# Cross attention of a decoder layer: memory's parts beside w_out, key pair 0 ahead of the queries, w_co's first unit by heads, X2's squares in wide operations after w_co

## The chip, the cores and the metric

The kernel runs on one core of a Trainium2 chip. The metric is device time in microseconds (us) for one execution of the whole program, lower is better. Each of the core's engines runs its own queue of instructions in order: PE (matrix multiplies into banks of PSUM), DVE (vector operations), ACT (activation functions, casts), POOL (general vector operations, and a DMA queue of its own), and SP, which here only issues DMA transfers. An engine waits where an operand isn't ready or a buffer isn't free.

## The reference

One inference step of one decoder layer, for 256 prompt rows and 8 sample rows (one new row each) that share all weights, in fp32:

```python
# 1. mixer: sliding-window attention and an SSD (Mamba-2) group, then one output projection
x = x + concatenate([attn, ssd], -1) @ w_out               # 3072 -> 2048
# 2. cross attention, 4 heads of 128, into 256 memory tokens
h = rms_norm(mem, g_mem)                                   # 256 x 2048 (prompt only)
k = rms_norm((h @ w_ck).reshape(b, m, 4, 128), ck_norm_g)
v = (h @ w_cv).reshape(b, m, 4, 128)
q = rms_norm((rms_norm(x, g_cross) @ w_cq).reshape(b, t, 4, 128), cq_norm_g)
p = softmax(einsum('bqhd,bshd->bhqs', q, k) * 128 ** -0.5)
x = x + einsum('bhqs,bshd->bqhd', p, v).reshape(b, t, 512) @ w_co
# 3. ConvFFN
u = causal_dwconv(rms_norm(x, g_ffn) @ w_up, ...)          # 2048 -> 2 x 5632, width 3
x = x + (silu(gate) * val) @ w_down
```

The sample rows attend to cached memory keys and values of their own (`cache_mem_k`, `cache_mem_v`). Memory's keys and values, the SSD states and other caches are outputs too.

## The kernel before

**Tiling.** Activations lie transposed: 128 features on the partitions, 264 columns (256 prompt rows, then 8 sample rows), 16 such blocks for the 2048 features. Every fp32 product is three matmuls (`mm3`, lines 100 to 103): of the weights' high part with the activations' high part (L101) and low part (L102), and of the weights' low part with the activations' high part (L103). The high part is a rounded cast, the low part what it leaves. `split` (L91 to L98) makes both for activations: the high part on ACT, the low part on DVE.

**Weights.** `weights` (L69) loads 1 MB from HBM into one of two `wraw` slots over SP's queue; of each half, ACT casts `whi` (L86) and DVE subtracts `wlo` (L87), into four slots each, so the engines can be two units ahead of PE. `proj` (L105) runs some units of weights into `nb` PSUM banks and then hands each bank to an evaluation, which frees it. Of the banks, three are `mm`, two `t`, and `s`, `x` and `y` have one each.

**Order.** The program is written in one sequence; a scheduler decides at build time in which order each engine's queue gets its instructions, and `high_priority` marks weights and evaluations. After that the order is fixed.

**The stretch of the change**, in the order of the program (L736 to L979):
- `w_out` in two halves: eight units against `AT` (attention), then eight projections of two units against `Y` (the SSD group). Each evaluation of the second half adds to the residual `res`, splits the sum into `X1` (16 blocks, `x1h` and `x1l`) and adds its square to `accx` (`sumsq`, L173: ACT squares, POOL adds).
- `memory_norm` (L738): loads the memory into four `mraw` tiles of 128x1024, squares and adds its 16 blocks one by one (`accm`, by `sumsq`), and takes the inverse root mean squares `rmc` (`col_rms`, L188, whose small matmuls are at L192).
- After `w_out`: the 16 blocks of the memory are split into `M` (`mh`, `ml`).
- `q_pair(0)`, `q_pair(1)`: the queries of two heads each, with their per-head norms (`head_rms`, L798, small matmuls at L804), and the sample rows' queries sent to HBM (`dram_q`). `k_pair(0)` and `k_pair(1)`: memory's keys (`kx`).
- `sample_logits(i)`: the sample rows of head pair i. Cached keys `kt` are multiplied by the queries, which come back from HBM on all partitions (`qb`); the exponentials `es` go to HBM (`dram_p`).
- `probs(h)`: softmax of head h for the prompt rows (`e`, divided by `den` on POOL, transposed into `pts`).
- `v_pair(i)`: memory's values (`vx`). `sample_out(i)`: the exponentials come back on all partitions (`pb`), cached values `vt` (three slots) are multiplied by them; the result goes into the sample columns of `OH` and `OL`. `out_head(h)`: probabilities times values, into head h's prompt columns of `OH` and `OL`.
- `w_co`: four units of 1 MB, each with four output blocks (`nb=4`, all in `mm` banks) over the four heads. The evaluation adds to `res`, splits into `X2` (`x2h`, `x2l`) and adds the square to `accx2`.
- `r2`, from `accx2` (`total`, L181), which the evaluations of `w_up` need: each multiplies its bank by `r2` into `u` (L1033).
- Beside `w_up`, the SSD states of the sample rows are updated (`new_state`): 16 tiles `hn` of eight 128x128 updates, each in three slots: loaded over SP's queue, scaled on ACT (L1005), updated on DVE (L1006), and stored by POOL's queue. `w_up` and `w_dn` fill the time from 671 us to the end.

Of the kernel before, what the change touches and what calls it, by code (L numbers as in the profile page):

```python
# [14 lines left out]
D = 2048  # L15
# [32 lines left out]
def hybrid_decoder_step_kernel(ctx: ExitStack, tc: tile.TileContext, I, O):  # L48
# [56 lines left out]
    def proj(units, acts, evac, n=T, nb=2, tag="mm"):  # L105

        outs = [psum(tag) for _ in range(nb)]
        for ui, (src, (ah, al)) in enumerate(zip(units, acts)):
            parts = src if isinstance(src, list) else weights(src)
            for pi, (wh, wl) in enumerate(parts):  # L110
                wh = wh.rearrange("p (k c) -> p k c", c=128 * nb)
                wl = wl.rearrange("p (k c) -> p k c", c=128 * nb)
                nk = wh.shape[1]
                for m in range(nb):
                    for k in range(nk):
                        kk = pi * nk + k
                        mm3(outs[m][:, :n], wh[:, k, m * 128:(m + 1) * 128], wl[:, k, m * 128:(m + 1) * 128],
                            ah[:, kk, :n], al[:, kk, :n],
                            ui == 0 and kk == 0, ui == len(units) - 1 and kk == nk * len(parts) - 1)
        for m in range(nb):  # L120
            with tc.high_priority():
                evac(m, outs[m][:, :n])
# [615 lines left out]
    def memory_norm():  # L738
        cr = ExitStack()
        xp = cr.enter_context(tc.tile_pool(name="xp", bufs=1))  # L740
        accm = small.tile([128, T], F32, tag="acc", bufs=1, name="accm")[:, :TP]
        mraw = []
        for h in range(4):
            mr = xp.tile([128, 4, TP], F32, tag="mr", name="mraw", bufs=4)
            nc.sync.dma_start(out=mr, in_=I["memT"][:, 4 * h:4 * h + 4, :])
            for k in range(4):
                sumsq(accm, mr[:, k, :], h + k == 0, TP)
            mraw.append(mr)
        rmc = col_rms(accm, "rmc")
        return cr, xp, mraw, rmc  # L750

# [10 lines left out]
    cr, xp, mraw, rmc = memory_norm()  # L762
# [12 lines left out]
    r1c = col_rms(accx, "r1c")  # L775

    ax2 = cpool.tile([128, 8, 2], F32, name="ax2")
    V.tensor_copy(out=ax2, in_=accx[:, TP:T].unsqueeze(2).broadcast_to([128, 8, 2]))
    p = psum("y")
    PE.matmul(p[0:16, 0:1], ax2.rearrange("p b m -> p (b m)"), ones[:, 0:1], start=True, stop=True)  # L780
    r1s = cpool.tile([16, 2], F32, name="r1s")
    rms(r1s[:, 0:1], p[0:16, 0:1], D)
    V.tensor_tensor(out=r1s[:, 1:2], in0=r1s[:, 0:1], in1=r1s[:, 0:1], op=ALU.mult)


    M = [(T3(apool, 8, F32R, "B", f"mh{h}", 4), T3(apool, 8, F32R, "B", f"ml{h}", 4)) for h in range(2)]
    for k in range(KB):
        split(M[k // 8][0][:, k % 8, :TP], M[k // 8][1][:, k % 8, :TP], mraw[k // 4][:, k % 4, :], pc("g_mem", k))

    qx = xp.tile([128, 4, TP], F32, tag="mr", name="qx", bufs=4)  # L790
    kx = xp.tile([128, 4, TP], F32, tag="mr", name="kx", bufs=4)
    vx = xp.tile([128, 2, 512], F32, tag="mr", name="vx", bufs=4)
    pts = [xp.tile([128, 2, 2, 256], F32, tag="mr", name="pt0", bufs=4), xp.tile([128, 2, 2, 256], F32, name="pt1")]
    OH = xp.tile([128, 4, T], F32R, name="oh")
    OL = xp.tile([128, 4, T], F32R, name="ol")
# [14 lines left out]
    def q_pair(i):  # L810
# [18 lines left out]
        for m in range(2):  # L829
            P.tensor_copy(out=qq[:, :, m], in_=sqs[m][:, TP:T])  # L830
# [10 lines left out]
    def k_pair(i):  # L841
# [10 lines left out]
        proj([I["w_ck"][2 * i], I["w_ck"][2 * i + 1]], M, ev, n=TP)  # L852
# [36 lines left out]
    def sample_out(i):  # L889
        pbs = []  # L890
        rd = xp.tile([128, 8, 2], F32, tag="rd", name="rd", bufs=2)
        for hf in range(2):
            t = T3(apool, 8, tag="A", name=f"pb{i}{hf}", bufs=4)
            pb = t.rearrange("p a t -> p (a t)")[:, 0:2056].rearrange("p (r s) -> p r s", r=8)
            nc.sync.dma_start(out=pb, in_=dram_p[i][8 * hf:8 * hf + 8, :].partition_broadcast(128))
            V.reciprocal(out=rd[:, 4 * hf:4 * hf + 4, :], in_=pb[:, :, 256].rearrange("p (b m) -> p b m", m=2))
            pbs.append(pb)
        for bb in range(4):
            vt = xp.tile([128, 2, 2, 256], F32, tag="kt", name="vt", bufs=3)
            nc.sync.dma_start(out=vt, in_=I["mvT"][i, bb])  # L900
            for b in range(2):
                for m in range(2):
                    row = 4 * bb + 2 * b + m
                    V.scalar_tensor_tensor(out=vt[:, b, m, :], in0=vt[:, b, m, :], scalar=1.0, in1=pbs[row // 8][:, row % 8, 0:256],
# [4 lines left out]
    def probs(h, f):  # L909
# [13 lines left out]
        P.tensor_tensor(out=e3, in0=e3, in1=den.unsqueeze(2).broadcast_to([128, 2, 256]), op=ALU.mult)  # L923
# [7 lines left out]
    def v_pair(i):  # L931
        pv = [psum("mm") for _ in range(2)]
        for u in range(2):
            parts = [w.rearrange("p (k c) -> p k c", c=256) for hl in weights(I["w_cv"][2 * i + u]) for w in hl]
            nk = parts[0].shape[1]
            for k in range(8):
                wh, wl = parts[2 * (k // nk)], parts[2 * (k // nk) + 1]
                for c in range(2):
                    cs = slice(c * 128, c * 128 + 128)
                    mm3(pv[c][:, 0:256], M[u][0][:, k, cs], M[u][1][:, k, cs], wh[:, k % nk, :], wl[:, k % nk, :],  # L940
# [18 lines left out]
    for h in range(4):  # L959
        probs(h, fq[h // 2][0][:, :, h % 2])  # L960
# [9 lines left out]
    for u in range(4):  # L970
        def ev(m, pm, u=u):
            k = 4 * u + m
            x = res[k // 4][:, k % 4, :]
            V.tensor_tensor(out=x, in0=pm, in1=x, op=ALU.add)  # L974
            split(X2[k // 8][0][:, k % 8, :], X2[k // 8][1][:, k % 8, :], x, pc("g_ffn", k))
            sumsq(accx2, x, k == 0)
        proj([I["w_co"][u]], [(OH, OL)], ev, nb=4)
# [262 lines left out]
```

## Time and profile before

| | |
|---|---|
| median of 3 runs | 1458.18 us (1455.09 to 1459.53) |
| the profiled execution's own time | 1454.73 us |
| its span in the trace | 1453.0 us |
| mean granted clock of PE | 0.993 |
| first half of w_out ends, second begins | 453.4 us |
| queries begin (w_cq) | 549.0 us |
| w_co begins, ends | 636.1, 670.3 us |
| w_up begins | 671.2 us |

All later times in the profile count from the start of the span. A row of the view of windows gives, for a stretch, the busy time of each engine with the number of its instructions, the clock granted to PE, the share of the DMA engines' time and the rate. A row of the view of waits gives who waited for whom: total, times, longest. In a row of the timeline, the first two numbers are start and length, then engine, line, operation, `output<-inputs`, size and count, and in brackets how long the engine had been idle ahead of it and what ended that.

### The profile page before, as it was taken

What the parts mean: (1) busy time and instruction counts of PE and PEld (TensorE: products, weight loads), DVE (VectorE), ACT (ScalarE), POOL (GpSimd) and SP (SyncE); (2) the same over time, 40 slices, a digit from 0 to 9 for tenths busy, and PEclk for the clock granted to TensorE, in tenths of its full rate; (3) what the DMA queues carried; (4) which work ended last, traced back from release to release, by engine and by line L of the source; (5) the groups of instructions that cost most, each with busy time, mean ns of one, the idle gap of its engine ahead of it and who ended that gap; (6) DMA issues with size and microseconds to landing.
All of it is one profiled execution on the core that took longest, in us unless ns stands there. A gap on an engine that the chain in (4) does not pass through costs nothing.

```text
span 1453.0 us, 28695 instructions
## 1 busy us (share of the span) xinstructions
PE 1415.6 (97%) x11453; PEld 1386.2 (95%) x11453; DVE 1068.6 (74%) x2025; ACT 787.9 (54%) x1316; POOL 191.4 (13%) x366
## 2 busy tenths in 40 slices
PE   6999999999999999989899999999999999999999
PEld 5999899999999999979899999999999999999999
DVE  7748878999966667779998665667566656665664
ACT  5557753568745456558786553454345434543442
POOL 4200011212224113016111010001000000000000
PEclk9999999999999999999999999999999999999999
DMA  6763346767675556966897455555555555455554
GB/s 229 281 198 136 119 156 207 243 233 258 220 275 196 191 180 208 342 249 252 322 350 300 175 176 186 189 176 178 183 189 176 176 185 190 176 176 184 191 189 147
DMA packets 59223, 304.66 MB, mean 210 GB/s; under 512 B 8848, under 2 KB 13904, under 8 KB 29392
## 3 DMA queue, kind: packets, MB, share of 16 engines
q1 hardware_dynamic: 53584, 283.94, 55.7%
q0 software_dynamic: 5504, 18.88, 3.5%
q8 instruction: 90, 1.47, 0.4%
q14 instruction: 45, 0.37, 0.1%
HBM read 287.06 MB, written 16.28 MB: 209 GB/s over the span
## 4 chain that ended last, share of the span: by engine, by line
PE 74%; DVE 14%; DMA 5%; issue 3%; ACT 3%; POOL 1%; SPq 0%; ACTq 0%; DVEq 0%; POOLq 0%
PE mm L101 16%; PE mm L102 16%; PE mm L103 16%; PE t L103 7%; PE t L101 7%; PE t L102 7%; DVE wlo L87 4%; DMA wraw<-in_w_in_dram 2%; DMA wraw<-in_w_ck_dram 1%; DMA wraw<-in_w_out_dram 1%; DVE h L651 1%; ACT whi L86 1%; POOL accm L179 1%; PE s L407 1%; DVE hn L1006 1%
## 5 line engine op out<-in xcount | busy, mean ns | idle before, releaser
L86 ACT CAST whi<-wraw 128x1024 fp32r<-128x1024 f32 x444 | 461.3, 1049 | 528.5 <-PE mm L102 302.0
L87 DVE TENSOR_TENSOR wlo<-wraw,whi 128x1024 fp32r<-128x1024 f32 x448 | 551.8, 1236 | 260.7 <-ACT whi L86 255.1
L103 PE MATMUL t<-x2h,wlo 128*128 128x264 f32 x704 | 198.2, 285 | 3.7 <-DVE wlo L87 3.7
L101 PE MATMUL t<-x2h,whi 128*128 128x264 f32 x704 | 200.2, 285 | 1.5 <-ACT whi L86 1.5
L101 PE MATMUL mm<-x2h,whi 128*128 128x264 f32 x704 | 199.4, 284 | 0.8 <-DVE res L974 0.6
L102 PE MATMUL t<-x2l,whi 128*128 128x264 f32 x704 | 199.8, 285 | 0.0
L102 PE MATMUL mm<-x2l,whi 128*128 128x264 f32 x704 | 199.2, 284 | 0.0
L102 PE MATMUL mm<-hl,whi 128*128 128x264 f32 x704 | 198.8, 283 | 0.0
L103 PE MATMUL mm<-x2h,wlo 128*128 128x264 f32 x704 | 197.2, 284 | 1.6 <-DVE wlo L87 1.6
L103 PE MATMUL mm<-hh,wlo 128*128 128x264 f32 x704 | 198.6, 283 | 0.0
L101 PE MATMUL mm<-hh,whi 128*128 128x264 f32 x704 | 196.9, 284 | 0.0
L103 PE MATMUL mm<-xh,wlo 128*128 128x264 f32 x608 | 174.0, 290 | 3.0 <-DVE wlo L87 3.0
L101 PE MATMUL mm<-xh,whi 128*128 128x264 f32 x608 | 176.2, 292 | 0.0
L102 PE MATMUL mm<-xl,whi 128*128 128x264 f32 x608 | 175.5, 290 | 0.0
L103 PEld LDWEIGHTS t<-x2h,wlo 128*128 128x128 f32 x704 | 131.9, 189 | 4.1 <-DVE wlo L87 4.1
L101 PEld LDWEIGHTS t<-x2h,whi 128*128 128x128 f32 x704 | 133.2, 189 | 1.7 <-ACT whi L86 1.7
L101 PEld LDWEIGHTS mm<-x2h,whi 128*128 128x128 f32 x704 | 132.5, 188 | 1.1 <-issue 0.8
L102 PEld LDWEIGHTS t<-x2l,whi 128*128 128x128 f32 x704 | 133.2, 189 | 0.0
L103 PEld LDWEIGHTS mm<-x2h,wlo 128*128 128x128 f32 x704 | 131.1, 188 | 2.0 <-DVE wlo L87 2.0
L102 PEld LDWEIGHTS mm<-x2l,whi 128*128 128x128 f32 x704 | 132.5, 188 | 0.0
L102 PEld LDWEIGHTS mm<-hl,whi 128*128 128x128 f32 x704 | 132.4, 188 | 0.0
L103 PEld LDWEIGHTS mm<-hh,wlo 128*128 128x128 f32 x704 | 132.2, 188 | 0.0
(414 smaller groups left out, 3088.0 us busy)
## 6 DMA issues: line engine op xcount, KB each, us to landing
wraw<-in_w_up_dram SPq DMA_DIRECT2D x88, 1024.0 KB, 4.9
wraw<-in_w_in_dram SPq DMA_DIRECT2D x52, 1024.0 KB, 5.2
wraw<-in_w_dn_dram SPq DMA_DIRECT2D x44, 1024.0 KB, 4.9
wraw<-in_w_out_dram SPq DMA_DIRECT2D x24, 1024.0 KB, 4.9
h<-in_h_dram POOLq DMA_DIRECT2D x32, 256.0 KB, 4.1
hn<-in_h_dram SPq DMA_DIRECT2D x16, 512.0 KB, 6.8
out_state_s_dram<-hn POOLq DMA_DIRECT2D x16, 512.0 KB, 6.6
pb<-dram_p SPq DMA_DIRECT2D x4, 1028.0 KB, 10.0
```

The source lines that it names most:

```text
L86: S.copy(out=hi, in_=x)
L87: V.tensor_tensor(out=lo, in0=x, in1=hi.bitcast(F32), op=ALU.subtract)
L101: PE.matmul(out, wh, xh, start=start, stop=False)
L102: PE.matmul(out, wh, xl, start=False, stop=False)
L103: PE.matmul(out, wl, xh, start=False, stop=stop)
L179: P.tensor_tensor(out=acc, in0=acc, in1=sq[:, :w], op=ALU.add)
L407: PE.matmul(s3, qT[:, j, c * 128:c * 128 + 128], kbd[:, pp, :, 0:nk], start=True, stop=True)
L651: V.tensor_tensor(out=h0, in0=h0, in1=cb, op=ALU.mult)
L1006: V.scalar_tensor_tensor(out=h[:, b, :], in0=bbs[g][:, b, :], scalar=xds[:, k, b:b + 1], in1=h[:, b, :], op0=ALU.mult, op1=ALU.add)
```

## The change

It has five parts, all between `w_out` and the start of `w_up`; the work of PE's matmuls stays the same, except for their order.

1. **Memory.** Its squares are taken in four ACT operations of 128x1024 (`msq`), added on DVE, beside the first half of `w_out`. Its parts (`mh`, `ml`) are made there too and not after the second half. `rmc` comes four projections later.
2. **Keys and queries.** `k_pair(0)` comes ahead of `r1c` and the queries; `probs` of heads 0 and 1 ahead of `k_pair(1)`, `sample_logits(1)` after it.
3. **Places and engines.** `qx`, `kx`, `vx` and `pts` lie in three flat tiles; the copies `qq` and the division by `den` move from POOL to DVE.
4. **w_co.** Its unit 0 runs with the heads outside and the four outputs inside, in two `mm` and two `t` banks; units 1 to 3 use `mm` and `t` in turn.
5. **X2's squares.** In place of 16 squares with POOL's adds beside `w_co`, four ACT squares of 128x1056 after it, added on DVE.

```diff
+    def memory_sum():
+        sl = [xp.tile([128, 4, TP], F32, tag="kt", name="msq", bufs=3) for _ in range(3)]
+        for h in range(3):
+            S.activation(out=sl[h], in_=mraw[h], func=AF.Square)
+        V.tensor_tensor(out=sl[0], in0=sl[0], in1=sl[1], op=ALU.add)
...
+    def memory_parts(k):
+        split(*mem_hl(k), mraw[k // 4][:, k % 4, :], pc("g_mem", k))
...
         proj([w_out[8 + 2 * i], w_out[9 + 2 * i]], Y, ev, tag="t" if i % 2 else "mm")
+        if i == 0:
+            accm = memory_sum()
+        if i == 3:
+            rmc = col_rms(accm, "rmc")
+        if i > 0:
+            for k in range(3 * i - 3, min(3 * i, KB)):
+                memory_parts(k)
...
-            P.tensor_copy(out=qq[:, :, m], in_=sqs[m][:, TP:T])
+            V.tensor_copy(out=qq[:, :, m], in_=sqs[m][:, TP:T])
...
-        P.tensor_tensor(out=e3, in0=e3, in1=den.unsqueeze(2).broadcast_to([128, 2, 256]), op=ALU.mult)
+        for c in range(2):
+            V.tensor_scalar(out=e3[:, c, :], in0=e3[:, c, :], scalar1=den[:, c:c + 1], scalar2=None, op0=ALU.mult)
...
+    k_pair(0)
+    r1c = col_rms(accx, "r1c")
...
     fq = [q_pair(i) for i in range(2)]
-    k_pair(0)
-    for i in range(2):
-        sample_logits(i, fq[i][1])
+    sample_logits(0, fq[0][1])
+    for h in range(2):
+        probs(h, fq[0][0][:, :, h])
     k_pair(1)
...
-    for h in range(4):
-        probs(h, fq[h // 2][0][:, :, h % 2])
+    sample_logits(1, fq[1][1])
+    for h in range(2, 4):
+        probs(h, fq[1][0][:, :, h - 2])
...
+    outs = [psum(t) for t in ("mm", "mm", "t", "t")]
+    for pi, (wh, wl) in enumerate(weights(I["w_co"][0])):
+        for k in range(2):
+            h = 2 * pi + k
+            for m in range(4):
+                mm3(outs[m][:, :T], wh[:, k, ms], wl[:, k, ms], OH[:, h, :], OL[:, h, :], h == 0, h == 3)
...
+    S.activation(out=a2, in_=res[0], func=AF.Square)
+    for c in range(1, 4):
+        S.activation(out=b2, in_=res[c], func=AF.Square)
+        V.tensor_tensor(out=a2, in0=a2, in1=b2, op=ALU.add)
+    V.tensor_tensor(out=a2[:, 0:2, :], in0=a2[:, 0:2, :], in1=a2[:, 2:4, :], op=ALU.add)
+    V.tensor_tensor(out=accx2, in0=a2[:, 0, :], in1=a2[:, 1, :], op=ALU.add)
```

The scheduler puts these instructions elsewhere than the text has them. ACT's queue beside `w_out`'s first half, from the split of `ysam` on, before the change (`sq` are the memory's squares, `whi` the casts of `w_out`'s units 4, 5 and later):

```order
L94 CAST yh_2214<-ysam 128x8x8
L86 CAST whi<-wraw 128x1024 x2
L178 ACTIVATE sq<-mraw 128x256 x2
L86 CAST whi<-wraw 128x1024 x3
L170 ACT_TABLE_LOAD
L170 ACTIVATE ry<-y,eps 128x264
```

And of the changed kernel, at the same place:

```order
L94 CAST yh_2214<-ysam 128x8x8
L86 CAST whi<-wraw 128x1024 x2
L765 ACTIVATE msq<-mraw 128x1024
L97 ACTIVATE mh_5493<-mraw,par 128x256 x4
L765 ACTIVATE msq<-mraw 128x1024
L97 ACTIVATE mh_5493<-mraw,par 128x256 x4
L86 CAST whi<-wraw 128x1024
L765 ACTIVATE msq<-mraw 128x1024
L97 ACTIVATE mh_5494<-mraw,par 128x256 x8
L767 ACTIVATE msq<-mraw 128x1024
L86 CAST whi<-wraw 128x1024 x4
L171 ACT_TABLE_LOAD
```

All four squares and all 16 high parts of the memory now stand ahead of the casts of unit 5, and two squares and eight parts ahead of the second cast of unit 4.

SP's queue of transfers around the sample rows of head pair 1, from their exponentials (`dram_p`) on, before the change:

```order
L887 DMA dram_p<-es 16x257
L900 DMA vt<-in_mvT_dram 128x1024 x3
L895 DMA pb_7757<-dram_p 128x2056
L895 DMA pb_7760<-dram_p 128x2056
L74 DMA wraw<-in_w_co_dram 128x2048
L900 DMA vt<-in_mvT_dram 128x1024
L74 DMA wraw<-in_w_co_dram 128x2048
L900 DMA vt<-in_mvT_dram 128x1024
```

And of the changed kernel:

```order
L901 DMA dram_p<-es 16x257
L911 DMA vt<-in_mvT_dram 128x1024 x2
L74 DMA wraw<-in_w_co_dram 128x2048
L990 DMA out_mem_k_dram<-qk 128x1024
L911 DMA vt<-in_mvT_dram 128x1024
L74 DMA wraw<-in_w_co_dram 128x2048
L907 DMA pb_7103<-dram_p 128x2056
L907 DMA pb_7104<-dram_p 128x2056
L999 DMA out_mem_v_dram<-vp 128x1024
L74 DMA wraw<-in_w_co_dram 128x2048
L911 DMA vt<-in_mvT_dram 128x1024
```

The broadcast `pb` of pair 1 now stands behind a load of `w_co` and the store of the keys, and only one load of `vt` is left behind it.

DVE's queue around the last split of `X2` and up to the first evaluations of `w_up` (`r` is `r2`, L1033 the evaluations `u`), before the change:

```order
L98 SCALAR_TENSOR_TENSOR x2l_7804<-res_4958,par,x2h_7803 128x264 x2
L87 TENSOR_TENSOR wlo<-wraw,whi 128x1024 x2
L171 RECIPROCAL r_8150<-r_8150 128x264
L1006 SCALAR_TENSOR_TENSOR hn<-bb,xds,hn 128x128 x9
L1033 TENSOR_TENSOR u<-mm,r_8150 128x264
```

And of the changed kernel, where `st` holds the squares of `X2` (of the 72 updates `hn` that it has ahead of `u`, 33 stand in these rows):

```order
L1062 SCALAR_TENSOR_TENSOR hn<-bb,xds,hn 128x128 x9
L1031 TENSOR_TENSOR st_8071<-st_8071 128x1056
L87 TENSOR_TENSOR wlo<-wraw,whi 128x1024 x4
L1062 SCALAR_TENSOR_TENSOR hn<-bb,xds,hn 128x128 x3
L1032 TENSOR_TENSOR st_8071<-st_8071 128x528
L1062 SCALAR_TENSOR_TENSOR hn<-bb,xds,hn 128x128 x12
L1033 TENSOR_TENSOR accx_7774<-st_8071 128x264
L1062 SCALAR_TENSOR_TENSOR hn<-bb,xds,hn 128x128 x9
L87 TENSOR_TENSOR wlo<-wraw,whi 128x1024 x3
L172 RECIPROCAL r_8083<-r_8083 128x264
L87 TENSOR_TENSOR wlo<-wraw,whi 128x1024
L1089 TENSOR_TENSOR u<-mm,r_8083 128x264
```

The reciprocal of `r2`, and with it every evaluation of `w_up`, now stands behind the state updates of nine tiles; SP's queue issues those tiles' loads ahead of `w_up`'s first units rather than behind three of them.

More of the change, by code (lines that the diff above doesn't have):

```diff
@@ L774, in hybrid_decoder_step_kernel, with flat @@
         proj([w_out[8 + 2 * i], w_out[9 + 2 * i]], Y, ev, tag="t" if i % 2 else "mm")
[L775 to L795, printed above, removed]
+        if i == 0:
[5 more added lines that the diff above has]
+                memory_parts(k)
+    def flat(name):
+        return T3(apool, 8, tag="B", name=name, bufs=4).rearrange("p a t -> p (a t)")
+    qk, vp, pp1 = flat("qk"), flat("vp"), flat("pp1")
+    qx = qk[:, 0:1024].rearrange("p (h t) -> p h t", h=4)
+    kx = qk[:, 1024:2048].rearrange("p (h t) -> p h t", h=4)
+    vx = vp[:, 0:1024].rearrange("p (c n) -> p c n", c=2)
+    pts = [t.rearrange("p (m a q) -> p m a q", m=2, a=2) for t in (vp[:, 1024:2048], pp1[:, 0:1024])]
     os_ = xp.tile([128, 4, 8], F32, name="os_")
```

90 lines of the change are left out of this document (58 added, 32 removed).

## The prediction

> **What bounds the kernel now.** I read the page first (busy shares, chain of waits), then the stages in the table of windows, then PE's waits over the stretch that the change touches.
>
> ```profile
> span 1453.0 us, 28695 instructions
> PE 1415.6 (97%) x11453; PEld 1386.2 (95%) x11453; DVE 1068.6 (74%) x2025; ACT 787.9 (54%) x1316; POOL 191.4 (13%) x366
> PE 74%; DVE 14%; DMA 5%; issue 3%; ACT 3%; POOL 1%; SPq 0%; ACTq 0%; DVEq 0%; POOLq 0%
> ```
>
> PE is busy for 97% and carries 74% of the chain that ended last; the change takes no matmul away. So it can win only idle time or low-clock time of PE: 1453.0 − 1415.6 = 37 us in the whole span. Where that lies, by stage:
>
> ```profile
> 420.00:455.00 35.00, 34.79 (x283) 34.17 (x282) 18.33 (x22) 17.88 (x28) 14.02 (x14) 1.00 0.79 286
> 455.00:460.00 5.00, 3.13 (x27) 2.92 (x26) 3.34 (x6) 2.72 (x5) 1.88 (x2) 1.00 0.47 154
> 590.00:617.00 27.00, 25.28 (x199) 24.94 (x198) 21.86 (x109) 16.52 (x29) 1.14 (x1) 0.94 0.91 357
> 617.00:636.00 19.00, 18.32 (x139) 17.37 (x138) 16.74 (x56) 11.49 (x24) 2.08 (x2) 1.00 0.86 343
> 636.00:653.00 17.00, 12.50 (x70) 10.29 (x68) 9.40 (x24) 7.53 (x18) 1.18 (x2) 0.90 0.44 156
> 653.00:671.00 18.00, 17.57 (x144) 17.31 (x143) 17.43 (x27) 13.74 (x28) 11.59 (x12) 1.00 0.39 125
> 671.00:703.00 32.00, 27.87 (x211) 27.41 (x212) 30.04 (x57) 25.90 (x56) 14.66 (x21) 0.95 0.88 342
> ...
> 716.00:772.00 56.00, 56.00 (x463) 56.00 (x462) 53.86 (x128) 44.73 (x107) 9.87 (x27) 1.00 0.98 355
> ```
>
> Columns: length; busy of PE, PE's loads, DVE, ACT, POOL with instruction counts; granted clock; DMA share; GB/s. Undisturbed, PE issues a matmul in 56.0/463 = 0.121 us; by that rate it loses 1.7 us at 455–460 (5 − 27 × 0.121), 2.9 beside the key pairs (590–617, clock 0.94), 2.2 at 617–636, 8.5 around the heads (636–653, clock 0.90) and 6.5 at the start of w_up (671–703). That is the most there is to win. Two columns matter later: **DVE is full at 653–703** (17.43 of 18, 30.04 of 32) and **DMA is nearly full at 590–617** (0.91). What PE waited for:
>
> ```profile
> PE t L103 <- DVE wlo L87: 3.7, 2, 2.4
> PE y L192 <- POOL accm L179: 1.9, 1, 1.9
> PE y L804 <- ACT sq L849: 1.7, 1, 1.7
> ```
>
> **Place 1, the memory's squares and parts beside w_out.** Removed: PE's wait for POOL's accm at 455 (1.9); the sum is now DVE's and its matmul comes four projections later. Added in front of the weight casts of units 4 and 5: four ACT squares of 128x1024, 16 mh of 128x256, and on DVE 16 ml and the adds.
>
> ```profile
> 433.97 2.00 ACT L86 CAST whi<-wraw 128x1024 fp32r<-128x1024 f32 x2 [6.27 <-DMA wraw<-in_w_out_dram]
> 550.07 3.30 ACT L97 ACTIVATE mh<-mraw,par 128x256 fp32r<-128x256 f32 x8
> 553.17 2.46 DVE L98 SCALAR_TENSOR_TENSOR ml<-mraw,par,mh 128x256 fp32r<-128x256 f32 x6
> 435.06 2.36 DVE L87 TENSOR_TENSOR wlo<-wraw,whi 128x1024 fp32r<-128x1024 f32 x2 [5.41 <-ACT whi L86]
> 436.34 0.39 PE L103 MATMUL t<-ath,wlo 128*128 128x264 f32 x1
> ```
>
> A mh costs 3.30/8 = 0.41 us, an ml 2.46/6 = 0.41. No ACT square this wide is in the trace; a 128x1024 cast has the same shape and takes 2.00/2 = 1.0, which I take (ends: 0.5, and 1.6 for four mh of a quarter its size). ACT's burden: 4 × 1.0 + 16 × 0.41 = 10.6 us, against the 6.27 us that it idled before unit 5's weights came. So unit 5's cast slips by 10.6 − 6.3 = 4.3, and PE starts that unit's main part at 436.34 + 4.3 = 440.6. DVE's 6.6 us of ml lie in the 5.41 us that it idled there and in the slip, and cost nothing more; if they come behind the casts instead, up to 2. Against it stand the 1.9 no longer waited at 455: +2.4. After a wait as long as this the clock may be low for a while (0 to 2 us): I take 0.6, **together +3.0** (ends 0 and +6). The DVE adds stand behind the casts that PE needs first. SP's later weight loads start later, since slots come free later, but PE comes as much later too.
>
> **Place 2, cross attention** (times without place 1's shift). Removed: PE's 1.7 behind ACT's exponential at 590, with the low clock behind it, 2.9 in all (key pair 0 comes first, and its L804 stands 15 matmuls into the queries, work that hides the squares), and part of the 2.2 at 617–636, now under the v pairs; I take 1. POOL's e times 1/den becomes two DVE operations. But the 96 matmuls of key pair 0 (two outputs, 16 blocks, three each), 11.6 us, now ahead of the queries, put the sample rows' chain 11.6 us later: q, dram_q, qb, es, dram_p, pb, vt, and last their columns of OH.
>
> ```profile
> 580.61 0.32 SPq L828 DMA_DIRECT2D dram_q<-qr  x1
> 608.46 0.33 SPq L887 DMA_DIRECT2D dram_p<-es  x1
> 610.89 6.41 SPq L900 DMA_DIRECT2D vt<-in_mvT_dram  x3
> 617.40 0.86 SPq L895 DMA_DIRECT2D pb<-dram_p  x2
> pb<-dram_p SPq DMA_DIRECT2D x4, 1028.0 KB, 10.0
> vt<-in_mvT_dram SPq DMA_DIRECT2D x8, 512.0 KB, 8.7
> dram_p<-es SPq DMA_DIRECT2D x2, 16.1 KB, 6.2
> 643.28 0.17 DVE L95 TENSOR_TENSOR ol<-os__6680,oh 128x16 fp32r<-128x16 f32 x1
> 670.29 0.28 PE L103 MATMUL mm<-oh,wlo 128*128 128x264 f32 x1
> ```
>
> (Last column of the DMA rows: median us to landing.) Pair 1's dram_p goes from 608.46 to 608.5 + 11.6 = 620.1, lands 6.2 later: its pb is issued at 626.3 at the earliest, lands near 626.3 + 10 = 636; the last vt, behind it in SP's queue, lands about 641, its four products and the split take 2.5: **OH's columns of heads 2 and 3 are ready at about 644**, as now (643.28). PE itself comes 3.9 us sooner: w_co, which starts at 636.1 now, starts at 632, and heads 0 and 1 of unit 0 with the small matmuls carry it to some 636. Then it waits until 644: one wait of about 8 us in place of the several that make up the 8.5. Left are 168 of w_co's 192 matmuls, 168 × 0.121 = 20.3, and 2 us for low clock. w_co ends at 644 + 20.3 + 2 = 666.3 against 670.3 now: **−4.0** (ends: −12 if the columns come 8 sooner, 0 if they come 4 later).
>
> A rule of the Trainium skill, "TensorE: Matmul & The Clock Gate", section "Why this matters for your kernels", says idle gaps over about 3 us drop the clock. The trace shows clock 0.90 at 636–653 with no single wait above 2 us, and 1.00 at 455–460 with one of 1.9: so short waits cost clock here at times, which the rule would not have. By the rule, place 1's wait of 4 us and place 2's of 8 both cost clock, and the waits of 1 to 3 us in place 3 none: the sum would be 1 us lower.
>
> **Place 3, X2's sum of squares and the start of w_up.** Removed: 15 POOL adds (off PE's path), 16 ACT squares of 128x264. Added on DVE: three 128x1056 adds, a half and a quarter of one, ahead of r2, and with r2 so late, 72 hn updates ahead of it instead of 9. w_up's first four u need r2; PE cannot begin its third pair of outputs before them, as its banks are taken.
>
> ```profile
> L98 DVE SCALAR_TENSOR_TENSOR x2l<-res,par,x2h 128x264 fp32r<-128x264 f32 x16 | 11.3, 727 | 0.2 <-ACT x2h L97 0.2
> 651.79 0.48 DVE L98 SCALAR_TENSOR_TENSOR x2l<-res,par,x2h 128x264 fp32r<-128x264 f32 x1
> 650.76 1.11 DVE L974 TENSOR_TENSOR res<-mm,res 128x264 f32<-128x264 f32 x3 [0.60 <-PE mm L103]
> 689.07 2.97 DVE L1006 SCALAR_TENSOR_TENSOR hn<-bb,xds,hn 128x128 f32<-128x128 f32 x11
> L171 DVE RECIPROCAL r<-r 128x264 f32<-128x264 f32 x1 | 1.8, 1789 | 0.0
> L95 DVE TENSOR_TENSOR atl<-attn,ath 128x1056 fp32r<-128x1056 f32 x2 | 2.5, 1246 | 0.0
> ```
>
> DVE's queue from the first res of w_co to the fourth u, by pitch (an instruction starts before the one ahead has ended: three res in 1.11, one alone 0.42, so 0.345 each): 16 res, 5.6; 16 x2l at 0.40, 6.4 (0.48 alone as at 651.79, against 0.73 on average now, beside POOL's adds, which go); 15 wlo at 1.14, 17.1; 72 hn at 0.26, 18.7; the adds at a 128x1056 subtract's 1.25 and by size, 3 × 1.2 + 0.6 + 0.35 = 4.5; reciprocal 1.8; four u 1.4. Sum 55.5. It starts when unit 0 is done, at 644 + 3 = 647, so the first pair of u is there at 647 + 54.8 = 701.8, if nothing stops DVE. PE could have w_up's first 192 matmuls done by 666.3 + 23.2 = 689.5, so it waits for wlo's and then for u, 12 us in all. By 703 PE has issued 211 matmuls now (the row of 671–703), 2 of them r2's: 17 beyond the 192. In the changed kernel 701.8 + 17 × 0.121 + 1 for low clock = 704.9. So the 4.0 of place 2 are given back, and 1.9 more: **place 3 is +5.9** (ends: 0 if DVE has done hn before 647 or does x2l and wlo first, +12 below).
>
> **Place 4, after it.**
>
> ```profile
> PE mm L103 <- DVE wlo L87: 1.6, 2, 1.0
> PE t L103 <- DVE wlo L87: 1.2, 1, 1.2
> L1006 DVE SCALAR_TENSOR_TENSOR hn<-bb,xds,hn 128x128 f32<-128x128 f32 x32 | 10.0, 377 | 0.0
> ```
>
> The first two rows are PE's waits from 703 to 785, 2.8 us and with the slow issue behind them some 4.4; the third counts hn updates before 705. Of 128, 96 are left behind that point now, 56 after the change: DVE, full there (53.86 of 56 us), has 40 × 0.26 = 10 us less. I leave 1 us of the losses: **−3.4** (ends −4.4 and 0).
>
> **Sum.** +3.0 − 4.0 + 5.9 − 3.4 = +1.5 us on the profiled execution's own 1454.73 (span 1453.0 and 1.7 around it) gives 1456.2. The median of the runs shown, 1458.18, lies 3.45 above that execution: 1459.7.
>
> **Rivals.**
> *Faster: the waits really go.* If pair 1's pb is issued at 618 rather than 626, because dram_p is late through SP's queue and DVE now and not through q (28 us lie between dram_q and dram_p of pair 1, of which the transfers explain a part), PE's 8 us wait goes, and DVE starts its queue 8 us sooner. For it: SP stood still for 6.41 us right there. Against it: DMA shares of 0.91 and 0.86. It wins the 8 of the wait, and 2 of clock: 1459.7 − 10 = 1450.
> *Slower: hn's round trips hold r2.* Ahead of r2, DVE needs nine hn tiles of eight updates; three slots hold them, and each goes in, is scaled, updated and stored before the next.
>
> ```profile
> hn<-in_h_dram SPq DMA_DIRECT2D x9, 512.0 KB, 7.9
> out_state_s_dram<-hn POOLq DMA_DIRECT2D x6, 512.0 KB, 4.6
> ```
>
> (640 to 720.) A round takes 7.9 + 4.6, 2.1 for its eight updates and as much on ACT, 17 us; the third round's load, from a first one near 645, lands at 645 + 2 × 17 + 8 = 687, and if each waits 3 to 5 us more in SP's queue behind w_up's, at 695 to 700. The ninth tile decides from 692 on, since 2 us of hn, four wlo and r2 follow it. At 699 it adds 7 us: 1467.
> *It moves waits only:* that is the forecast itself, pair 1's chain last in place 2 and DVE in place 3.
>
> **How the numbers follow.** The forecast has a chance of 0.45 (own range 1455 to 1464), faster rival 0.27, slower rival 0.28. A measurement of this kernel can tell some 0.3% (4.4 us) from no change: 1453.8 to 1462.6. Of the forecast 0.42 lies inside and 0.03 above; of the slower rival 0.02 inside. Faster 0.27, same 0.44, slower 0.29. Range: from 1449 (place 2 at −13) to 1468 (place 3 at +12 and the clock's cost), which leaves out about 2 in 10.
>
> **What would show it.** Place 1: PE's wait at 455 gone, one of 4 us for whi or wlo before 441. Place 2: no wait at L804, one of some 8 us for the sample columns of OL ahead of unit 0's heads 2 and 3. Place 3: DVE busy throughout between 650 and 700, r2's reciprocal near 700, PE's longest wait there for u. Place 4: wlo waits after 703 under 1 us. Wrong if pb of pair 1 lands before 630, if DVE has gaps before r2, or if PE's waits of place 3 sum to under 4 us.

## The result, and the profile after

The changed kernel takes 1478.76 us (median of 4 runs, 1474.09 to 1480.36) against 1456.91 for the kernel before: a ratio of 1.0137, 95% interval [1.0121, 1.0153]. It is 22 us slower, where 1.5 us slower was forecast, and outside the range. The page of the changed kernel's profiled execution (1480.36 us) begins:

```profile
span 1478.5 us, 28611 instructions
PE 1423.2 (96%) x11453; PEld 1392.4 (94%) x11453; DVE 1071.4 (72%) x2047; ACT 784.9 (53%) x1292; POOL 147.8 (10%) x328
PE 70%; DVE 12%; DMA 8%; ACT 5%; issue 3%; POOL 0%; SPq 0%; ACTq 0%; DVEq 0%; POOLq 0%
```

PE executes the same 11453 matmuls; POOL and ACT have less to do, as intended. The chain that ended last now runs over DMA for 8% of the span (5% before) and over PE for 70% (74%). To see where the time went, the program is cut where PE does the same work in both kernels: A from `w_out`'s first matmul to its last, B from there to `w_co`'s last, C on to `w_up`'s 205th, D on to its 801st (each length is the difference of two starts in PE's timeline):

| us | A, w_out | B, cross attention | C, first w_up | D |
|---|---|---|---|---|
| before | 143.1 | 121.5 | 32.1 | 75.6 |
| after | 146.9 | 134.0 | 36.8 | 79.5 |
| difference | +3.8 | **+12.5** | +4.6 | +3.8 |
| forecast | +3.0 | −4.0 | +5.9 | −3.4 |

The sum is +24.7; ahead of A, where nothing was changed, this execution was 1.7 us late besides. A and C are about as long as forecast (for C, see place 3 below, the reason is another). B and D have the wrong sign. The view of windows of the changed kernel (columns as before):

```profile
420.00:455.00 35.00, 31.11 (x234) 29.76 (x233) 28.96 (x46) 22.60 (x35) 0.00 (x0) 0.95 0.75 270
...
560.00:590.00 30.00, 30.00 (x252) 29.65 (x251) 13.76 (x25) 14.57 (x27) 0.00 (x0) 1.00 0.50 173
590.00:617.00 27.00, 25.84 (x210) 24.99 (x209) 22.08 (x137) 19.05 (x36) 0.00 (x0) 1.00 0.85 287
...
640.00:660.00 20.00, 12.50 (x57) 10.23 (x55) 10.21 (x36) 7.40 (x17) 0.00 (x0) 0.83 0.88 343
660.00:680.00 20.00, 15.48 (x109) 15.27 (x110) 15.75 (x45) 11.94 (x29) 7.84 (x9) 0.83 0.60 224
680.00:700.00 20.00, 16.15 (x116) 15.34 (x115) 20.00 (x44) 20.00 (x49) 1.60 (x3) 0.91 0.77 278
```

And two rows of the same view of the kernel before:

```profile
560.00:590.00 30.00, 29.74 (x248) 29.01 (x247) 18.80 (x90) 14.58 (x31) 6.80 (x4) 1.00 0.81 270
640.00:660.00 20.00, 17.19 (x111) 15.44 (x112) 12.32 (x27) 9.82 (x21) 5.82 (x6) 0.91 0.32 111
```

At 560 to 590 PE is now undisturbed (252 matmuls against 248), but the DMA engines work for only 0.50 of the time instead of 0.81. At 640 to 660 PE issues 57 matmuls against 111, with the DMA engines at 0.88 instead of 0.32. The transfers of the sample rows start later: between 560 and 590 SP issued loads of `qb` and `kt` for both pairs before the change, and only the first of `qb` after it; pair 1's `pb` and `vt` now run at 640 to 660, where PE waits for what becomes of them. What PE waits for there (view of waits, 640 to 700 us):

```profile
PE mm L101 <- ACT ohl L94: 7.4, 1, 7.4
PE mm L103 <- DVE wlo L87: 2.9, 3, 1.6
PE mm L101 <- ACT whi L86: 2.1, 1, 2.1
```

The longest wait is for `ohl` of line 94, the sample columns of heads 2 and 3, as forecast, but it ends at 663.19, not at 644 (649.5 with the 5.5 us by which PE was late ahead of it). SP's queue shows why (timeline of SP, some rows left out):

```profile
628.86 0.33 SPq L901 DMA_DIRECT2D dram_p<-es  x1
629.29 5.09 SPq L911 DMA_DIRECT2D vt<-in_mvT_dram  x2
635.19 0.33 SPq L74 DMA_DIRECT2D wraw<-in_w_co_dram  x1
635.85 0.34 SPq L990 DMA_DIRECT2D out_mem_k_dram<-qk  x1
638.97 0.33 SPq L911 DMA_DIRECT2D vt<-in_mvT_dram  x1
640.18 0.33 SPq L74 DMA_DIRECT2D wraw<-in_w_co_dram  x1
640.60 1.42 SPq L907 DMA_DIRECT2D pb<-dram_p  x2
...
657.36 0.33 SPq L911 DMA_DIRECT2D vt<-in_mvT_dram  x1
...
664.27 1.51 SPq L1058 DMA_DIRECT2D hn<-in_h_dram  x3
...
673.52 0.33 SPq L74 DMA_DIRECT2D wraw<-in_w_up_dram  x1
```

`dram_p` of pair 1 goes at 628.86, and `pb` 11.7 us after it, which is 5.5 more than the 6.2 of its landing that the prediction counted: it stands behind two `vt` loads, a `w_co` load, the store of the keys, another `vt` and another `w_co` load. The last `vt` needs the slot of one that is multiplied by `pb`, so it goes only at 657.36. Then follow the state tiles `hn`, at 664, while `w_co` still runs until 688; before the change the first of them went at 671.49, after `w_co`'s end. On DVE, the sample columns, the first result of `w_co` and r2's reciprocal:

```profile
663.17 0.17 DVE L95 TENSOR_TENSOR ohl<-os__6629,ohl 128x16 fp32r<-128x16 f32 x1 [0.27 <-ACT ohl L94]
667.12 0.43 DVE L1006 TENSOR_TENSOR res<-mm,res 128x264 f32<-128x264 f32 x1 [3.77 <-PE mm L103]
...
729.34 1.80 DVE L172 RECIPROCAL r<-r 128x264 f32<-128x264 f32 x1 [0.57 <-ACT r L171]
```

r2's reciprocal comes 41 us behind `w_co`'s last matmul (688.26); before it was 12 us (682.18 behind 670.29). Yet PE never waited for r2. The first output of `w_up`'s third pair went, from 722.42 on, into the one bank that was left, and the matmul that ends C ran before the first evaluation `u` (rows of PE, then of DVE):

```profile
722.42 0.39 PE L101 MATMUL mm<-x2h,whi 128*128 128x264 f32 x1 [0.81 <-ACT whi L86]
...
725.01 0.28 PE L101 MATMUL mm<-x2h,whi 128*128 128x264 f32 x1
```

```profile
732.13 0.42 DVE L1089 TENSOR_TENSOR u<-mm,r 128x264 f32<-128x264 f32 x1
```

In C, PE waited 7.0 us in all (4.5 before), and mostly for parts of the weights, `whi` and `wlo`. These came late because the state tiles stand ahead of them. SP waits for tiles to be stored before it can load the next ones, with `w_up`'s loads behind these, and ACT waits for the weights (views of waits of SP, 660 to 735 us, and of ACT, 686 to 735):

```profile
SPq L1058 <- DMA out_state_s_dram<-hn: 42.3, 8, 8.8
```

```profile
ACT whi L86 <- DMA wraw<-in_w_up_dram: 8.9, 3, 5.2
```

### The profile page after: what moved, and what is told of

Same layout as the page of the kernel before. It is cut to its first block, busy times and chain, and to the rows that moved or that the text cites. A ratio compares the mean times of both kernels' runs of the same rounds, so it can differ in the third digit from the quotient of the medians.

```text
span 1478.5 us, 28611 instructions
## 1 busy us (share of the span) xinstructions
PE 1423.2 (96%) x11453; PEld 1392.4 (94%) x11453; DVE 1071.4 (72%) x2047; ACT 784.9 (53%) x1292; POOL 147.8 (10%) x328
## 4 chain that ended last, share of the span: by engine, by line
PE 70%; DVE 12%; DMA 8%; ACT 5%; issue 3%; POOL 0%; SPq 0%; ACTq 0%; DVEq 0%; POOLq 0%
PE mm L101 16%; PE mm L102 16%; PE mm L103 16%; PE t L101 7%; PE t L103 7%; PE t L102 7%; DVE wlo L87 4%; DMA wraw<-in_w_in_dram 2%; ACT whi L86 2%; DMA wraw<-in_w_up_dram 1%; DVE h L652 1%; DMA wraw<-in_w_cv_dram 1%; DVE hn L1062 1%; DMA qb<-dram_q 1%; DVE c L529 1%
## 5 line engine op out<-in xcount | busy, mean ns | idle before, releaser
L103 PE MATMUL mm<-x2h,wlo 128*128 128x264 f32 x704 | 200.3, 286 | 4.1 <-DVE wlo L87 4.1
```

The lines of the kernel that those rows point to most:

```text
L103: PE.matmul(out, wl, xh, start=False, stop=stop)
```

## The experiments

Each was measured beside the kernel before on the same chip, whose median was 1457 to 1459. Lengths of the stretches are as in the table above, each from one profiled execution.

**1. Is it the state tiles ahead of r2?** OH and OL lay in cross attention's pool (`xp`) before; in the changed kernel they lie elsewhere, so that `xp` is free, and the tiles of `w_up`'s pool `fp` may be loaded into its place, before `w_co` ends.

```diff
+    V.tensor_copy(out=os_[:, 0, 0:1], in_=res[3][:, 3, 0:1])
     st2 = T3(apool, 8, tag="A", name="st2", bufs=4)
```

> The changed kernel with one tiny DVE copy more, which reads the last residual block after w_co and writes a tile of the cross-attention pool, so that this pool's memory, which w_up's state tiles take over, is not free before w_co ends, as it was before the change (OH and OL lay in it). By the built order 14 state updates instead of 72 then stand ahead of r2 on DVE, and four loads of w_up ahead of the first state tile on SP. Theory A (OH and OL left the pool, the state tiles could be loaded before w_co's end, and their updates and loads hold r2 and w_up's weights): 10 to 14 us faster than the changed kernel's 1478.8, so 1465 to 1469, with r2's reciprocal less than 12 us behind the last matmul of w_co (40 us behind it in the changed kernel). Rival B (the wide squares and adds behind w_co are themselves the chain that makes r2 late): within 3 us of 1478.8, r2 as late as now.

1469.12 us, ratio 1.0073 [1.0050, 1.0097]: 9.7 us faster than the changed kernel. C fell from 36.8 to 31.7, below the 32.1 before the change, and D from 79.5 to 77.3. Its rows on SP and DVE:

```profile
692.15 0.33 SPq L74 DMA_DIRECT2D wraw<-in_w_up_dram  x1
...
693.83 1.52 SPq L1059 DMA_DIRECT2D hn<-in_h_dram  x3
```

```profile
708.91 1.79 DVE L172 RECIPROCAL r<-r 128x264 f32<-128x264 f32 x1
```

The state tiles go after `w_up`'s first loads again, and r2 comes 21 us behind `w_co`'s last matmul (688.35), half of what it was, though not the 12 expected. Rival B falls: the wide squares are all still there. Theory A holds in the main, with a gain just under the 10 us named. Since PE didn't wait for r2, what was won is that the weights' parts come sooner: the moved tile let the state tiles in ahead of them.

**2. SP's queue, or DVE's?**

```diff
-            nc.sync.dma_start(out=hns[k], in_=I["h0"][k])
+            nc.gpsimd.dma_start(out=hns[k], in_=I["h0"][k])
```

> The changed kernel with the loads of the state tiles on POOL's queue instead of SP's; on DVE all 72 updates stay ahead of r2. Theory A1 (the loss lies in w_up's weight loads, which stand behind state tiles that wait for a slot in SP's queue): 6 to 10 us faster than the changed kernel, 1469 to 1473, and w_up's loads come without gaps. Theory A2 (the loss lies in DVE's in-order queue, where 72 updates and their tiles' round trips stand ahead of r2): within 4 us of 1478.8, and the reciprocal still behind the ninth tile's landing.

1481.35 us, 1.0175 [1.0142, 1.0207]: no gain. r2 is as late as without it (41 us behind `w_co`), behind 64 updates (eight more stand between it and the first `u`):

```profile
722.35 2.39 DVE L1062 SCALAR_TENSOR_TENSOR hn<-bb,xds,hn 128x128 f32<-128x128 f32 x8 [2.11 <-ACT hn L1061]
...
727.12 1.80 DVE L172 RECIPROCAL r<-r 128x264 f32<-128x264 f32 x1 [0.57 <-ACT r L171]
```

This is what A2 named: DVE's in-order queue waits for the tiles' round trips (the brackets: idle for ACT's scaling of one), and a free SP queue alone doesn't help. ACT's queue is in order as well, and now waits for the tiles where it had waited for weights (686 to 735 us):

```profile
ACT hn L1061 <- DMA hn<-in_h_dram: 14.5, 5, 4.3
```

It isn't a clean test of SP's share, since on POOL's queue the tiles' loads also hold up their stores (see the end).

**3. Place 2: `pb` off SP's queue.** (For `pb_pool_hold`, with the edit of 1 as well.)

```diff
-            nc.sync.dma_start(out=pb, in_=dram_p[i][8 * hf:8 * hf + 8, :].partition_broadcast(128))
+            nc.gpsimd.dma_start(out=pb, in_=dram_p[i][8 * hf:8 * hf + 8, :].partition_broadcast(128))
```

> The changed kernel with the broadcasts of the exponentials (pb) issued by POOL's queue, which has nothing else to do there, instead of SP's. Theory C (pair 1's pb stood 11.7 us behind its dram_p in SP's queue, behind vt loads that wait for a slot, a w_co load that waits for a slot, and the store of the keys): pb of pair 1 issues within 8 us of dram_p, the sample columns of heads 2 and 3 come 5 to 10 us sooner, PE's wait of 7.4 us for them shrinks by as much, and the time is 4 to 9 us below 1478.8 unless the state updates take it back. Rival D (the transfers themselves are the limit, DMA being nearly full): pb lands no sooner than 652 us, the time within 3 us of 1478.8.

> Both edits, pb on POOL's queue and the pool held until w_co's end. If A and C are right and independent, both gains add: 1478.8 less 10 to 14 and less 4 to 9, so 1456 to 1464, near the kernel before (1457). If A alone is right: 1465 to 1469. If neither: 1476 to 1481.

1480.76 us, 1.0159 [1.0129, 1.0188], and with the hold 1474.60, 1.0112 [1.0084, 1.0139], which lies between the ranges named. On POOL's queue `pb` left at 635.27, and by the DMA view (last column) took 8.2 us to land (median), near 644, ten us sooner than in the changed kernel:

```profile
635.27 1.05 POOL L907 DMA_DIRECT2D pb<-dram_p  x2 [18.16 <-PE y L962]
```

```profile
pb<-dram_p POOLq DMA_DIRECT2D x2, 1028.0 KB, 8.2
```

```profile
657.96 0.42 DVE L964 TENSOR_TENSOR ohl<-s,ohl 128x256 fp32r<-128x256 f32 x1 [3.46 <-ACT ohl L963]
...
658.41 0.38 DVE L915 SCALAR_TENSOR_TENSOR vt<-vt,pb 128x256 f32<-128x256 f32 x1
```

But its first product waited until 658.41, behind head 3's subtraction in DVE's queue. Neither theory was right as stated: `pb` landed well before D's 652, and C's gain didn't come. SP's queue is one of two fetters, and taking it off shows the other.

**4. The products first on DVE.** `pb_pool_hold`, and:

```diff
-        V.tensor_tensor(out=OL[:, h, :TP], in0=o[:, 0:256], in1=OH[:, h, :TP].bitcast(F32), op=ALU.subtract)
+        sub = V.tensor_tensor(out=OL[:, h, :TP], in0=o[:, 0:256], in1=OH[:, h, :TP].bitcast(F32), op=ALU.subtract)
+        if h >= 2:
+            tc.keep_in_program_order(sub)
```

> pb_pool_hold with head 2's and 3's OL subtraction pinned behind the products of the sample rows of pair 1 on DVE (in pb_pool those products stood behind the subtraction of head 3, 12 us after their pb had landed, and head 3's matmul stood behind PE's first w_co matmuls). Theory E (place 2's loss is DVE's in-order queue: the products wait for prompt heads, the prompt heads for PE, and PE then for the products): products start within 3 us of pb's landing, PE's wait for the sample columns falls from 7.4 to under 2 us, and the time falls 6 to 10 us below pb_pool_hold's 1474.6, to 1464 to 1469. Rival F (the last vt's load and the DMA set it): the wait stays above 5 us, the time within 3 us of 1474.6.

1472.67 us, 1.0101 [1.0078, 1.0123], and PE's wait still 5.9 us. The products now stood behind head 1's subtraction, and began at 654.50, so that theory E wasn't put to its test; the numbers are those named for F, for another reason. What the run shows is that the sample rows are bound to the prompt's heads at several places of DVE's queue. I left the single links there and undid the order that made them late.

**5. The order of keys and queries** (`hold_xp` with the sequence of before).

```diff
-    k_pair(0)
     r1c = col_rms(accx, "r1c")
...
     fq = [q_pair(i) for i in range(2)]
+    k_pair(0)
+    for i in range(2):
+        sample_logits(i, fq[i][1])
-    sample_logits(0, fq[0][1])
-    for h in range(2):
-        probs(h, fq[0][0][:, :, h])
     k_pair(1)
-    sample_logits(1, fq[1][1])
-    for h in range(2, 4):
-        probs(h, fq[1][0][:, :, h - 2])
+    for h in range(4):
+        probs(h, fq[h // 2][0][:, :, h % 2])
```

> hold_xp with keys and queries in the order of the kernel before (queries, key pair 0, both sample pairs, key pair 1, four heads). Theory G (key pair 0 ahead of the queries puts the sample chain of pair 1 late, which is place 2): dram_p of pair 1 leaves 12 us sooner, 10 us or more of place 2 go, 1456 to 1460. Rival H (the loss is in how unit 0 of w_co and the heads interleave): within 4 us of hold_xp's 1469, with PE's wait for the sample columns still over 5 us.

1459.01 us, 1.0011 [0.9991, 1.0031]: 10 us less than `hold_xp`, and B is 119.7, 1.9 under the kernel before. `dram_p` goes 15 us sooner than in `hold_xp` (630.47 there), and the sample columns are ready at 650.2 (666.3 there):

```profile
615.35 0.32 SPq L901 DMA_DIRECT2D dram_p<-es  x1
...
626.74 0.86 SPq L907 DMA_DIRECT2D pb<-dram_p  x2
```

This is theory G's forecast, and PE's wait for the sample columns is gone. `pb` stands 11.4 us behind `dram_p` here too: the queue was about as long, but all of it ended sooner. The edit undoes three moves at once, key pair 0's, that of heads 0 and 1 and that of `sample_logits(1)`; experiment 8 moves key pair 0 alone, half of the way.

**6. Unit 0 of `w_co` by heads, or the wide squares?** Both on `hold_xp` (of each edit, the lines taken out are left out here). The first gives `w_co` back its loop of before, the second X2's squares:

```diff
...
+    for u in range(4):
+        proj([I["w_co"][u]], [(OH, OL)], lambda m, pm, u=u: x2_ev(4 * u + m, pm), nb=4)
...
```

```diff
         split(X2[k // 8][0][:, k % 8, :], X2[k // 8][1][:, k % 8, :], x, pc("g_ffn", k))
+        sumsq(accx2, x, k == 0)
...
```

> hold_xp with w_co's unit 0 by outputs and all units in mm banks, as before the change. Theory G (order of keys and queries): PE has 24 matmuls less to do before it waits, so 0 to 4 us slower than hold_xp, 1469 to 1473. Rival H (the interleaving by heads is what makes place 2 long): 4 us or more faster, below 1465.

> hold_xp with X2's squares as before the change (16 ACT squares, POOL adds, beside w_co). If the wide squares and adds behind w_co cost time of their own: r2's reciprocal, 16.5 us behind w_co's last evaluation in hold_xp, comes 3 to 5 us sooner, 1464 to 1467. If POOL's adds beside the splits cost DVE as much (they ran at 0.73 against 0.48 us beside them): within 2 us of 1469.

1467.21 us, 1.0072 [1.0049, 1.0095], and 1465.85, 1.0058 [1.0038, 1.0078]. Both intervals overlap with that of `hold_xp` ([1.0050, 1.0097]): neither gain is clear of noise, and PE's wait for the sample columns stays (7.8 and 8.1 us; 8.6 in `hold_xp`). So neither part is the main cause. The first time lies between the two ranges; the second lies where it was expected if the wide squares cost something, which experiments 9 and 10 don't bear out.

**7. Do places 2 and 3 add?** The order of before without the hold:

> The changed kernel with keys and queries in the order of before, and without the hold: the state tiles are still loaded early, 64 updates stand ahead of r2. If places 2 and 3 are separate losses that add (key pair 0 first, worth some 10 us; early state tiles, worth some 10): 1478.8 less 10, so 1466 to 1471, w_co ending as in undo_b_hold and r2 late again. If the sample columns' lateness also caused the state updates' harm: below 1463.

1464.41 us, 1.0056 [1.0035, 1.0077]: 14 us under the changed kernel, more than the 10 expected. B is 122.9, so place 2 is nearly mended; D is 83.7, the state tiles still in the way. The two single repairs are worth 9.7 and 14.4 us, both together (`undo_b_hold`) 19.8: two losses that can be repaired apart. That the sum falls short of 24.1 is within what the intervals leave open.

**8. DMA time, or the chain's latency?**

```diff
-    k_pair(0)
...
-    fq = [q_pair(i) for i in range(2)]
+    fq = [q_pair(0)]
+    k_pair(0)
+    fq.append(q_pair(1))
```

> hold_xp with key pair 0 between the two query pairs rather than ahead of both. Pair 0's sample chain starts 11.6 us sooner, pair 1's queries as late as in hold_xp. Theory G1 (DMA time: beside key pair 0 the DMA engines idled, 0.50 of their time at 560 to 590 us against 0.81 before, and the same transfers then had to run later, at 0.85 and more until 660): most of the loss of place 2 goes, 1459 to 1463. Theory G2 (latency: pair 1's queries come 11.6 us later, and its chain with them): 1466 to 1471, dram_p of pair 1 no sooner than 627.

1464.48 us, 1.0051 [1.0036, 1.0066], between the two. `dram_p` of pair 1 went at 621.06, nine sooner, yet `pb` only at 637.25, 16.2 behind it: SP's queue took a part of the gain back. PE's wait for the sample columns is the longest of all:

```profile
PE mm L101 <- ACT ohl L94: 11.4, 1, 11.4
```

Neither theory explains it alone, and this move wins under half of what experiment 5 won (4.6 of 10.1 us); how much of place 2 is DMA time and how much latency stays open.

**9. Place 1.** First, `undo_b_hold` with X2's squares as before, then that with the memory's ACT operations pinned behind what stands ahead of them in the program:

```diff
-            S.activation(out=sl[h], in_=mraw[h], func=AF.Square)
+            tc.keep_in_program_order(S.activation(out=sl[h], in_=mraw[h], func=AF.Square))
...
-        split(*mem_hl(k), mraw[k // 4][:, k % 4, :], pc("g_mem", k))
+        tc.keep_in_program_order(S.activation(out=hi, in_=x, func=AF.Copy, scale=g))
+        V.scalar_tensor_tensor(out=lo, in0=x, scalar=g, in1=hi.bitcast(F32), op0=ALU.mult, op1=ALU.subtract)
```

> undo_b_hold with X2's squares as before the change too: left of the change are the memory beside w_out, the places and engines, and w_co by heads. If the gain of 3 us that undo_e_hold showed over hold_xp holds here as well: 1455 to 1457, the time of the kernel before or a little less. If it doesn't add: 1458 to 1460.

> undo_be_hold with the memory's squares and high parts pinned on ACT behind the casts that stand ahead of them in the program, so that they come beside w_out's second half and not its first. Theory P (place 1's loss of 3 to 4 us is these operations ahead of the casts of units 4 and 5): 3 to 4 us less than undo_be_hold, no wait of PE between 424 and 457, and so 1451 to 1454, faster than the kernel before. If the second half has no room for them: no gain.

1462.87 us, 1.0031 [1.0014, 1.0047], slower than either expectation, and 1457.70, 1.0000 [0.9984, 1.0015]: the pin wins 5.2 us, a little more than expected, though the total stays above its range and the two intervals just touch. The traces have it in the right place: A is 4.9 us shorter with the pin. The pinned kernel's window:

```profile
420.00:455.00 35.00, 34.25 (x282) 34.04 (x281) 19.20 (x27) 12.16 (x14) 0.00 (x0) 1.00 0.75 272
```

PE issues 282 matmuls where the changed kernel issues 234 in the same stretch, and A falls to 141.3, 1.8 below the kernel before: POOL's wait is gone, and of the new ones 0.8 us is left.

**10. All three repairs, and the rest of the change kept.** `undo_b_hold` with the pin; and the same with `w_co` as in 6.

> undo_b_hold with the memory's operations pinned as in be_hold_pin: all three faults repaired (memory ahead of the casts, key pair 0 first, early state tiles), w_co by heads and the wide squares kept. If the three add, as be_hold_pin's 5 us under undo_be_hold suggest: undo_b_hold's 1459.0 less 3 to 5, 1454 to 1456, 1 to 4 us under the kernel before. If the rest of the change (w_co by heads, wide squares) costs by itself: 1457 or more.

> b_hold_pin with w_co's unit 0 by outputs again and all in mm banks. If the units by heads fill the wait for the last heads' parts (24 matmuls of 0.12, and waits at the heads of 8.5 us by windows before): 2 to 5 us slower than b_hold_pin. If not: within 1.5 us of it.

1453.13 us, 0.9958 [0.9942, 0.9974], and 1452.64, 0.9968 [0.9952, 0.9985]. Both beat both kernels, by 4.7 to 5.2 us under the kernel before. `w_co` by heads is worth nothing that can be measured here, and the wide squares don't cost: with them the kernel is 4.6 us faster than `be_hold_pin`, intervals apart. Where the gain over the kernel before lies stays open: the profiled executions of `b_hold_pin` (the slowest of its ten) and of the kernel before (one of its fastest) span the same 1453.0 us, and in the sum of A to D neither this gain nor that of the wide squares shows: 372.9 us in `b_hold_pin`, 372.3 before, 371.3 in `be_hold_pin`. Part 3 of the change (places and engines) is in all of these kernels; only its effect on the state tiles was tested, by the hold.

## Why the prediction was wrong, by its own steps

**Place 1 (+3.0; measured +3.8): right in mechanism, and close in size.** The rows of ACT and PE in the changed kernel:

```profile
435.12 3.29 ACT L97 ACTIVATE mh<-mraw,par 128x256 fp32r<-128x256 f32 x8
438.32 1.04 ACT L767 ACTIVATE msq<-mraw 128x1024 f32<-128x1024 f32 x1
439.26 3.87 ACT L86 CAST whi<-wraw 128x1024 fp32r<-128x1024 f32 x4
```

The wide square takes 1.04 us (1.0 taken), the cast of unit 5 begins at 439.26; the wait at 455 is gone. But there wasn't one wait of 4 us, as named: the waits between 420 and 460 us sum to 3.9, in pieces of which the longest is 1.3. Experiment 9 shows the place.

**Place 2 (−4.0; measured +12.5): this is where it failed.** That pair 1's chain comes last was right, and that one long wait for its columns takes the place of several (7.4 us against some 8). What failed is the step "its pb is issued at 626.3 at the earliest, lands near 626.3 + 10 = 636; the last vt, behind it in SP's queue, lands about 641". The earliest time was taken for the time, twice, and a landing in lighter traffic for the landing here. With the 5.5 us by which PE was late ahead of it, the step said 625.6 for `dram_p`, 631.8 for `pb`, 641.8 for its landing. `dram_p` went 3.3 later. `pb` went 8.8 later, 5.5 more, since it stood in SP's queue behind transfers of which several wait for slots, an order that was known. Even the kernel before, in the rows that the prediction shows, has `pb` 8.9 us behind `dram_p` and not 6.2. And in the changed kernel it took 13.4 us, not 10, to land, in a stretch where DMA is now nearly full:

```profile
pb<-dram_p SPq DMA_DIRECT2D x2, 1028.0 KB, 13.4
```

(DMA view, 636 to 655 us, last column.) That is 12.2 us in all, up to the landing. From there to the columns it took 1.5 more than the step has, since the last `vt` went only at 657.36, and from the columns to `w_co`'s end 25.1 us and not 22.3. With these 2.8, the 16.5 us between −4.0 and +12.5 are accounted for. The row of DMA share 0.91 was read as a bound on the *faster* rival, not as work that moves: what the DMA engines don't carry beside key pair 0 (0.50 at 560 to 590) they have to carry later (0.88 at 640 to 660). How much of the loss this makes wasn't separated from the chain's latency. Experiment 5 shows that the order of keys and queries is the cause; 3, 4 and 8 show that none of the single links tried is.

**Place 3 (+5.9; C measured +4.6): close in size by luck; the mechanism failed.** The step "PE cannot begin its third pair of outputs before them, as its banks are taken" is wrong: the pair has two outputs, one bank was left, and PE filled it from 722.42 to 733 while the first `u` came at 732.13. No wait of PE in C or D is for `u`. What made C longer are the waits for weights, 7.0 us against 4.5, and 33 matmuls at 0.22 us in place of 19. r2's own time was wrong too: its reciprocal came at 729, not near 700. Twenty of these us come from the stretches ahead, as DVE began at 667.12 and not at 647. From there to the reciprocal it took 62.2 us where the sum has 52.3. It was full for most of that (20.00 of 20 us at 680 to 700) but idled 6.4 us behind 716.5: 1.9 for the ninth tile's round trip, the *slower* rival's mechanism, and most of the rest for casts of `w_up`'s weights. The change behind it wasn't seen at all: OH and OL left the pool, and the scheduler could load state tiles before `w_co`'s end. The order showed the result (nine tiles ahead of r2); that this could be laid to one moved tile is what experiment 1 shows.

**Place 4 (−3.4; measured +3.8): failed.** Fewer updates were left behind the point, but `w_up`'s casts were still late: PE's waits for weights between 725 and 804.5 us, which is D, sum to 4.6 us, against 2.2 before in the same stretch:

```profile
PE mm L103 <- DVE wlo L87: 2.7, 3, 1.5
PE t L103 <- DVE wlo L87: 1.0, 1, 1.0
PE mm L101 <- ACT whi L86: 0.9, 1, 0.9
```

With the matmuls at 0.22 us behind them (14 against 3) this makes up most of the 3.8. A gain was counted from DVE's time in a stretch whose start had not been made sure of.

**The clock.** PE's rows behind its longest wait in the changed kernel:

```profile
663.19 0.81 PE L101 MATMUL mm<-ohl,whi 128*128 128x264 f32 x2 [7.44 <-ACT ohl L94]
...
666.66 0.42 PE L103 MATMUL mm<-ohl,wlo 128*128 128x264 f32 x1
666.88 0.42 PE L101 MATMUL mm<-ohl,whi 128*128 128x264 f32 x1
...
667.64 0.28 PE L102 MATMUL t<-ohl,whi 128*128 128x264 f32 x1
667.76 0.28 PE L103 MATMUL t<-ohl,wlo 128*128 128x264 f32 x1
```

Behind the wait of 7.4 us PE starts a matmul every 0.22 us for 4.3 us, then every 0.12: some 2 us are lost, as the sum of place 2 had it. The rule of the Trainium skill that the prediction weighed ("TensorE: Matmul & The Clock Gate", section "Why this matters for your kernels") agrees with this row. It doesn't cover the start of `w_up` in the same kernel: at 690 to 695 us the granted clock is 0.66, and matmuls start every 0.22 us, behind waits of which none is longer than 1.2 us.

## What to carry to other kernels

Where an engine's or a queue's order is fixed at build time, a transfer goes when its queue comes to it: count what stands ahead of it, and what slots these wait for, before calling a time its earliest. Moving a tile out of a pool frees the pool, and what is allocated there next may start early, be queued ahead, and hold the weights that stand behind it in the queues of SP, ACT and DVE. Projections that let an engine run without a wait are no gain if a longer chain, here the sample rows', starts later for them. Which instruction a stage waits for is read from its waits: the reciprocal here came 41 us behind `w_co`, and PE waited for something else.

## What the runs showed that was not expected

Loading the state tiles on POOL's queue made the stretch behind C longer, not shorter: D is 92.5 us in `hn_pool` against 79.5 in the changed kernel, with 72 updates ahead of the first `u` in both. A part of this may be that one execution, which took 1488.85 us where the other three took 1481.1 to 1481.6. POOL's queue shows a reason, which no run tested: between 682 and 734 us each load of a tile waits 4 to 10 us for an earlier tile's store to land, and the next store goes out only behind that load.
